# Row statistics of x from a token-major copy on ScalarE, first loads in another order, products of ones ahead of the data

## The chip, the cores and the metric

The kernel runs on one core of one Trainium2 chip. The metric is the device time in microseconds (us) of that core. A profile is one execution taken by the hardware profiler. Its span runs from the first to the last instruction. The engines are TensorE (PE, with its weight loads as PEld), VectorE (DVE), ScalarE (ACT), GpSimd (POOL) and SyncE (SP), which here only issues DMAs.

## The reference, cut to what matters

One block of a streaming encoder works on x of 256 tokens by 2048 features, in float32. Only its start bears on this change:

```
def rms_norm(x, g):
    y = x * lax.rsqrt(jnp.mean(x * x, axis=-1, keepdims=True) + EPS)
    return y * g

h = rms_norm(x, norm_mix_pre)
proj = h @ w_in                      # 2048 -> 20544 columns
q, k, v, z, xbc, dt, g_sb, g_ssd = split(proj)
```

After it come a stick-breaking attention, a Mamba-2 scan, their gated merge, an output projection, and a gated MLP with a width-3 convolution, each with the same kind of norm.

## The kernel before, in words

All large products are of float32 quality, made of three float32r passes: every operand is split into hi (the rounded value) and lo (the exact rest). The weights come as 713 units of 128 x 1024 floats (512 KB). For unit u SyncE loads `raw`u (five buffers), ScalarE casts it to `whi`u (line 63), VectorE subtracts to get `wlo`u (line 64), each with five buffers, and TensorE consumes both. So ScalarE can write `whi`u only when TensorE is done with unit u-5, and SyncE can load `raw`u only when VectorE is done with `wlo`(u-5).

The gain of the norm is multiplied into x, but 1/rms is applied to the products behind. So the first products need no statistics. x comes feature-major (`xT`) in four chunks of 512 KB, `x0` to `x3`. For each chunk ScalarE makes the hi half (line 188, four instructions of 128x256) and VectorE the lo half (line 189, four), both in `a`0 to `a`3. These and the splits of units 0 to 7 stand in a block whose order on ScalarE and VectorE is as written.

TensorE then runs `first`: four column tiles at once (`feat_mms`, lines 123 to 130), chunk by chunk. Per chunk two units are used. A unit gives 8 pairs of matmuls: hi weights by the 512 columns of hi and lo (line 112), lo weights by the 256 columns of hi (line 113). That makes 64 pairs for `first`, then 16 for each following column tile (`ps_xs`, `ps_bc`). After those come `ps_z` and the rest.

The statistics: GpSimd squares each chunk (line 197), adds the squares up (line 201) and folds them twice (line 203), nine instructions in all. Two small matmuls with ones (line 395, `ss_x`) sum over the partitions. `rsqrt_mean` (lines 237 to 242, names `rx_...`) makes 1/rms per token on VectorE and ScalarE. `tok_to_bc` spreads it over the partitions: `rx_dg` on VectorE, the matmul `rx_ps` (line 250) on TensorE behind the first `ps_xs` tile, and the copy `rstd_bc` (line 251) on VectorE. The convolutions (lines 311 to 315) and the dt path (lines 260 to 298) need `rstd_bc`.

Within one engine and one queue all work goes in order. Outside the blocks written as such, a scheduler sets that order.

Of the kernel before, what the change touches and what calls it, by code (L numbers as in the profile page):

```python
# [10 lines left out]
F32 = mybir.dt.float32  # L11
# [27 lines left out]
def block_kernel(ctx, tc, xT, xN, wts, vecs, rows, hvec, dskip, gain, out):  # L39
    """Float32 products run as three float32r passes on hi + lo halves (hi the rounded value, lo the  # L40
    exact rest) of both operands. Weights come in units [128, 8 x 128] and are split on chip."""
    nc = tc.nc
# [15 lines left out]
    def act_chunk(name):  # L58
        """four k tiles of an operand [feature, token]: hi and lo beside each other"""
        return slot(F32R, [4, 2, T], name)  # L60
# [5 lines left out]
    def lnexp():  # L66
        """the table set that serves both Ln and Exp"""
        tc.keep_in_program_order(nc.scalar.preload_act_table_set(LNEXP))

# [1 line left out]
    raw_t, spl_t = {}, {}  # L71
# [9 lines left out]
    def prep(parts=1):  # L81
        """split the next unit of weights, a part per step"""
        v = state["u"]
        state["u"] += 1
        if v not in raw_t:
            load(v)
        raw = raw_t.pop(v)
        hi = wspl.tile([P, 1024], F32R, tag="whi", name=f"whi{v}")
        lo = wspl.tile([P, 1024], F32R, tag="wlo", name=f"wlo{v}")
        spl_t[v] = (hi, lo)  # L90
        n = 1024 // parts
        for i in range(parts):
            w = slice(i * n, (i + 1) * n)
            split(hi[:, w], lo[:, w], raw[:, w])
            yield

    def unit(ahead=WBUFS - 2):
        """the next unit's hi and lo; the units after it are prepared ahead"""
        u = state["at"]
        state["at"] += 1  # L100
        while state["u"] <= min(u + ahead, n_units - 1):
            for _ in prep():
                pass
        return spl_t.pop(u)
# [4 lines left out]
    def feat_tile(ps, hi, lo, c, act, k, last):  # L109
        """one weight tile into out[feature 128, token 256]; columns 256: take hi x lo"""  # L110
        w = slice(c * P, (c + 1) * P)
        nc.tensor.matmul(ps, hi[:, w], act[:, k % 4, :, :].rearrange("p s t -> p (s t)"), start=(k == 0), stop=last)  # L112
        nc.tensor.matmul(ps[:, :T], lo[:, w], act[:, k % 4, 0, :], start=False, stop=last, skip_group_check=True)  # L113
# [9 lines left out]
    def feat_mms(acts, pss):  # L123
        """several column tiles together, so that each chunk of the operand is used for longer"""
        for kc in range(4):
            for i, ps in enumerate(pss):
                if i % 2 == 0:
                    hi, lo = unit()
                for k in range(4):
                    feat_tile(ps, hi, lo, 4 * (i % 2) + k, acts[kc], 4 * kc + k, 4 * kc + k == KT - 1)  # L130
# [5 lines left out]
    def tok_mm(acts, nk, name):  # L136
        """out[token 128, feature 512] for both token tiles"""
        pss = [mm_bank(f"{name}_{t}") for t in range(2)]
        for k in range(nk):
            if k % 2 == 0:  # L140
                hi, lo = unit()
            w = slice(k % 2 * 512, k % 2 * 512 + 512)
            for t in range(2):
                ah, al = (acts[k // 4][:, k % 4, s, t * P:(t + 1) * P] for s in range(2))
                nc.tensor.matmul(pss[t], ah, hi[:, w], start=(k == 0), stop=False)  # L145
                nc.tensor.matmul(pss[t], ah, lo[:, w], start=False, stop=False)  # L146
                nc.tensor.matmul(pss[t], al, hi[:, w], start=False, stop=(k == nk - 1))  # L147
            if k % 4 == 3:
                pump()
        return pss  # L150

# [1 line left out]
    bg = []  # L153
# [11 lines left out]

# [1 line left out]
    gpre = const.tile([P, KT], F32, name="gpre")  # L167
# [3 lines left out]
    for c in range(4):  # L171
        xr = slot(F32, [4, T], f"x{c}")
        nc.sync.dma_start(xr, xT[:, 4 * c:4 * c + 4, :])
        for u in range(2 * c, min(2 * c + 2, RBUFS)):
            load(u, 2 if u == 0 else 1)
        x_raw.append(xr)
    nc.sync.dma_start(vec, vecs[:, KT:])
    hv = const.tile([64, 2], F32, name="hv")
    nc.sync.dma_start(hv, hvec)

    with tc.manual_schedule(engines=ACT_DVE):
        lnexp()
        for c in range(4):
# [10 lines left out]
            a_ch.append(ac)  # L194
            sqc = slot(F32, [4 * T], f"xsq{c}")
            xf_c = x_raw[c].rearrange("p k t -> p (k t)")
            nc.gpsimd.tensor_tensor(sqc, xf_c, xf_c, op=ALU.mult)
            if c == 0:
                xsq = sqc
            else:  # L200
                nc.gpsimd.tensor_tensor(xsq, xsq, sqc, op=ALU.add)
    for n in (512, 256):
        nc.gpsimd.tensor_tensor(xsq[:, :n], xsq[:, :n], xsq[:, n:2 * n], op=ALU.add)

# [1 line left out]
    dsk = const.tile([P, 64], F32, name="dsk")  # L206
    nc.gpsimd.dma_start(dsk, dskip.partition_broadcast(P))
    ident = const.tile([P, P], F32, name="ident")
    make_identity(nc, ident)
    ones = const.tile([P, P], F32, name="ones")  # L210
    nc.gpsimd.memset(ones, 1.0)

# [20 lines left out]
    def rsqrt_mean(dst, src, n, name):  # L233
        """1 / sqrt(src / n + EPS) of [128, 2], with a Newton step"""
        v = tmp.tile([P, 2], F32, tag="rs_v", name=f"{name}_v")
        q = tmp.tile([P, 2], F32, tag="rs_q", name=f"{name}_q")
        nc.vector.tensor_scalar(v, src, 1.0 / n, EPS, op0=ALU.mult, op1=ALU.add)
        nc.scalar.activation(q, v, AF.Ln)
        nc.scalar.activation(dst, q, AF.Exp, scale=-0.5)
        nc.vector.tensor_tensor(q, dst, dst, op=ALU.mult)  # L240
        nc.vector.scalar_tensor_tensor(q, q, -0.5, v, op0=ALU.mult, op1=ALU.mult)
        nc.vector.scalar_tensor_tensor(dst, q, 1.5, dst, op0=ALU.add, op1=ALU.mult)

    def tok_to_bc(dst, src, pool, tag, name):
        """dst[p, token] = src[token] on every partition"""
        dg = tmp.tile([P, T], F32, tag="diag", name=f"{name}_dg", bufs=1)
# [5 lines left out]

# [1 line left out]
    cs_dram = dram.tile([64, T], F32, name="cs_dram")  # L254
# [44 lines left out]

# [1 line left out]
    y_ch = []  # L301
# [86 lines left out]
    def to_feat(ch, t, src, pool, tag, name):  # L388
        """src [token 128, 512] into the operand chunk ch [feature, token]"""
        split_chunk(ch, t, transposed(src, pool, tag, f"{name}_{t}"))  # L390

    def stats_x():
        ps = paux.tile([P, 512], F32, tag="aux", name="ss_x")
        for t in range(2):
            nc.tensor.matmul(ps[:, t:t + 1], xsq[:, t * P:(t + 1) * P], ones[:, 0:1], start=True, stop=True)
        rsqrt_mean(rstd_tok, ps[:, 0:2], 2048, "rx")

# [34 lines left out]

# [1 line left out]
    def gate(dst, name):  # L434
# [14 lines left out]

# [1 line left out]
    tmp = work.enter_context(tc.tile_pool(name="tmp_d", bufs=2))  # L451
# [10 lines left out]
    def attn_work(hg, qk, vt):  # L462
        """columns of a pair of heads: 0:512 = head, query (keys 0:128); 512:768 = head, query 128: (keys 128:)"""
        oc = act_chunk(f"o{hg}")
# [64 lines left out]

# [1 line left out]
    gat = [slot(F32, [2048], f"gat{t}") for t in range(2)]  # L531
# [21 lines left out]

# [1 line left out]
    xn = [slot(F32, [2048], f"xn{t}") for t in range(2)]  # L555
# [14 lines left out]
    class PostNorm:  # L570
        """the statistics of a normalised output that comes in four column blocks"""

# [77 lines left out]

# [1 line left out]
    r2 = const.tile([P, T], F32, name="r2")  # L652
# [74 lines left out]
def _m_tiles(w):  # L727
    """[k, n] -> [n / 128, 128, k / 128, 128]: a block per 128 columns, k's partition first"""
    k, n = w.shape
# [3 lines left out]
def _m_units(w):  # L733
    """units of 8 k tiles, column tile by column tile"""
    m = _m_tiles(w)
# [4 lines left out]
def _joint_units(w):  # L740
    """units of 4 k tiles of two column tiles, all column tiles' first, then all their second, ..."""
    m = _m_tiles(w)
# [4 lines left out]
def _n_units(w):  # L747
    """units of 2 k tiles by 512 columns: [n / 512, k / 256, 128, 1024]"""
    k, n = w.shape
# [3 lines left out]
def _cols(v):  # L753
    """[n] or [r, n] -> [128, n / 128 * r]: per partition, the r values of each tile"""
    v = v.reshape(-1, v.shape[-1])
# [50 lines left out]
```

## Time and profile before

| what | value |
|---|---|
| times of three runs | 2110.87, 2111.7, 2121.52 us (median 2111.7) |
| span of the profiled execution | 2109.0 us |
| TensorE busy | 2069.9 us (98%) |
| VectorE busy | 1399.9 us (66%) |
| ScalarE busy | 1154.5 us (55%) |
| GpSimd busy | 172.1 us (8%) |
| moved by DMA | 400.70 MB, mean 190 GB/s |

The profile gives a span and no other time for the execution that it records, so that span is set against the times of the runs. The busy shares are means over the whole program. The change lies in its first 50 us.

### The profile page before, as it was taken

What the parts mean: (1) busy time and instruction counts of PE and PEld (TensorE: products, weight loads), DVE (VectorE), ACT (ScalarE), POOL (GpSimd) and SP (SyncE); (2) the same over time, 40 slices, a digit from 0 to 9 for tenths busy, and PEclk for the clock granted to TensorE, in tenths of its full rate; (3) what the DMA queues carried; (4) which work ended last, traced back from release to release, by engine and by line L of the source; (5) the groups of instructions that cost most, each with busy time, mean ns of one, the idle gap of its engine ahead of it and who ended that gap; (6) DMA issues with size and microseconds to landing.
All of it is one profiled execution on the core that took longest, in us unless ns stands there. A gap on an engine that the chain in (4) does not pass through costs nothing.

```text
span 2109.0 us, 27916 instructions
## 1 busy us (share of the span) xinstructions
PE 2069.9 (98%) x10616; PEld 1761.4 (84%) x10616; DVE 1399.9 (66%) x1793; ACT 1154.5 (55%) x1538; POOL 172.1 (8%) x144
## 2 busy tenths in 40 slices
PE   7999999999999999999999999999999999999997
PEld 6788888888888888888888888788888888888886
DVE  8887877888544445555554566598788878854443
ACT  4776777677543334555556444475555555544442
POOL 4221012221000000000000021100000000000000
PEclk9999999999999999999999999999999999999999
DMA  6555555655655555555555746465565555566653
GB/s 237 178 186 189 201 185 176 210 171 181 191 195 193 193 196 188 182 170 170 170 174 183 272 162 208 150 239 190 190 189 191 190 190 190 190 230 199 200 192 108
DMA packets 108662, 400.70 MB, mean 190 GB/s; under 512 B 12368, under 2 KB 12624, under 8 KB 106480
## 3 DMA queue, kind: packets, MB, share of 16 engines
q1 hardware_dynamic: 104480, 377.97, 54.5%
q0 software_dynamic: 3328, 20.02, 2.7%
q8 instruction: 83, 1.36, 0.3%
q10 hardware_dynamic: 720, 0.93, 0.1%
q14 instruction: 51, 0.42, 0.1%
HBM read 394.61 MB, written 4.26 MB: 189 GB/s over the span
## 4 chain that ended last, share of the span: by engine, by line
PE 91%; DVE 3%; POOL 2%; issue 2%; ACT 1%; DMA 1%; SPq 0%; DVEq 0%; ACTq 0%; POOLq 0%
PE ps_fg L112 7%; PE ps_fv L112 7%; PE ps_qk L112 6%; PE ps_xs L112 5%; PE ps_fv L113 4%; PE ps_fg L113 4%; PE ps_fo L146 4%; PE ps_fo L147 4%; PE ps_fo L145 4%; PE ps_qk L113 3%; PE ps_ssd L147 3%; PE ps_ssd L145 3%; PE ps_ssd L146 3%; PE ps_xs L113 3%; PE ps_bc L112 2%
## 5 line engine op out<-in xcount | busy, mean ns | idle before, releaser
L64 DVE TENSOR_TENSOR wlo<-raw,whi 128x1024 fp32r<-128x1024 f32 (+1 forms) x715 | 908.8, 1276 | 601.1 <-ACT whi L63 600.7
L63 ACT CAST whi<-raw 128x1024 fp32r<-128x1024 f32 (+1 forms) x715 | 746.8, 1051 | 811.1 <-PE ps_fo L147 128.9
L112 PE MATMUL ps_fg<-h,whi 128*128 128x512 f32 x688 | 240.7, 391 | 0.0
L112 PE MATMUL ps_fv<-h,whi 128*128 128x512 f32 x688 | 240.5, 391 | 0.0
L113 PE MATMUL ps_fv<-h,wlo 128*128 128x256 f32 x688 | 192.7, 280 | 0.0
L113 PE MATMUL ps_fg<-h,wlo 128*128 128x256 f32 x688 | 192.7, 280 | 0.0
L112 PE MATMUL ps_qk<-a,whi 128*128 128x512 f32 x512 | 181.3, 398 | 0.0
L112 PE MATMUL ps_xs<-a,whi 128*128 128x512 f32 x464 | 162.9, 396 | 0.0
L112 PEld LDWEIGHTS ps_fg<-h,whi 128*128 128x128 f32 x688 | 128.7, 187 | 28.3
L112 PEld LDWEIGHTS ps_fv<-h,whi 128*128 128x128 f32 x688 | 128.7, 187 | 28.3
L113 PE MATMUL ps_qk<-a,wlo 128*128 128x256 f32 x512 | 143.5, 280 | 0.0
L147 PE MATMUL ps_fo<-whi,f 128*128 128x512 f32 x352 | 136.9, 389 | 0.0
L146 PE MATMUL ps_fo<-wlo,f 128*128 128x512 f32 x352 | 136.9, 389 | 0.0
L145 PE MATMUL ps_fo<-whi,f 128*128 128x512 f32 x352 | 136.9, 389 | 0.0
L113 PEld LDWEIGHTS ps_fg<-h,wlo 128*128 128x128 f32 x688 | 130.0, 189 | 0.0
L113 PEld LDWEIGHTS ps_fv<-h,wlo 128*128 128x128 f32 x688 | 130.0, 189 | 0.0
L113 PE MATMUL ps_xs<-a,wlo 128*128 128x256 f32 x464 | 129.0, 278 | 0.0
L112 PEld LDWEIGHTS ps_qk<-a,whi 128*128 128x128 f32 x512 | 96.1, 188 | 22.6
L145 PE MATMUL ps_z<-whi,a 128*128 128x512 f32 x256 | 103.6, 406 | 0.0
L112 PEld LDWEIGHTS ps_xs<-a,whi 128*128 128x128 f32 x464 | 87.0, 188 | 19.5
L146 PE MATMUL ps_z<-wlo,a 128*128 128x512 f32 x256 | 100.5, 393 | 1.0 <-DVE wlo L64 1.0
L147 PE MATMUL ps_z<-whi,a 128*128 128x512 f32 x256 | 100.1, 391 | 0.0
(283 smaller groups left out, 3853.3 us busy)
## 6 DMA issues: line engine op xcount, KB each, us to landing
raw<-wts SPq DMA_DIRECT2D x713, 512.0 KB, 3.8
csb<-cs_dram POOLq DMA_DIRECT2D x8, 1024.0 KB, 7.8
x<-xT SPq DMA_DIRECT2D x4, 512.0 KB, 9.0
csb<-gain POOLq DMA_DIRECT2D x8, 256.0 KB, 4.3
xn<-xN POOLq DMA_DIRECT2D x2, 1024.0 KB, 8.1
x_dram<-xn POOLq DMA_DIRECT2D x2, 1024.0 KB, 9.2
xe<-x_dram POOLq DMA_DIRECT2D x2, 1024.0 KB, 10.3
gfo<-rows POOLq DMA_DIRECT2D x4, 256.0 KB, 5.0
```

The lines of the kernel that those rows point to most:

```text
L63: nc.scalar.copy(hi, src)
L64: nc.vector.tensor_tensor(lo, src, hi.bitcast(F32), op=ALU.subtract)
L112: nc.tensor.matmul(ps, hi[:, w], act[:, k % 4, :, :].rearrange("p s t -> p (s t)"), start=(k == 0), stop=last)
L113: nc.tensor.matmul(ps[:, :T], lo[:, w], act[:, k % 4, 0, :], start=False, stop=last, skip_group_check=True)
L145: nc.tensor.matmul(pss[t], ah, hi[:, w], start=(k == 0), stop=False)
L146: nc.tensor.matmul(pss[t], ah, lo[:, w], start=False, stop=False)
L147: nc.tensor.matmul(pss[t], al, hi[:, w], start=False, stop=(k == nk - 1))
```

## The change

The nine squares and sums on GpSimd and the two `ss_x` matmuls go. Instead x is loaded once more, token-major (`xN`, two tiles `xt0`, `xt1` of 1 MB, 128 tokens each), on SyncE's queue. ScalarE squares each tile in place with a row sum (`accum_out`), one instruction of 128x2048 per tile. `rsqrt_mean` takes these sums.

The first loads come in another order: half of `x0`, half of unit 0, the other halves, unit 1, then `x1` and the rest as before. The loads of `vec` and `hv` are written behind the block of splits.

The constant `ones` is set by VectorE at the very start, and TensorE multiplies it by itself ten times (`wake`, float32, 128 columns each) into a bank that nobody reads. The diff also deletes comments, which moves line numbers; those parts are left out here.

```diff
...
+    ones = const.tile([P, P], F32, name="ones")
+    nc.vector.memset(ones, 1.0)
+    wake = paux.tile([P, 512], F32, tag="aux", name="wake")
+    for i in range(10):
+        nc.tensor.matmul(wake[:, :P], ones, ones, start=True, stop=True)
     gpre = const.tile([P, KT], F32, name="gpre")
     nc.scalar.dma_start(gpre, vecs[:, 0:KT])
     vec = const.tile([P, C_N - KT], F32, name="vec")
     a_ch, x_raw = [], []
     for c in range(4):
-        xr = slot(F32, [4, T], f"x{c}")
-        nc.sync.dma_start(xr, xT[:, 4 * c:4 * c + 4, :])
+        x_raw.append(slot(F32, [4, T], f"x{c}"))
+    raw0 = wraw.tile([P, 1024], F32, tag="raw", name="raw0")
+    raw_t[0] = raw0
+    for i in range(2):
+        nc.sync.dma_start(x_raw[0][:, 2 * i:2 * i + 2, :], xT[:, 2 * i:2 * i + 2, :])
+        nc.sync.dma_start(raw0[:, i * 512:i * 512 + 512], wts[0][:, i * 512:i * 512 + 512])
+    load(1)
+    for c in range(1, 4):
+        nc.sync.dma_start(x_raw[c], xT[:, 4 * c:4 * c + 4, :])
         for u in range(2 * c, min(2 * c + 2, RBUFS)):
-            load(u, 2 if u == 0 else 1)
-        x_raw.append(xr)
-    nc.sync.dma_start(vec, vecs[:, KT:])
-    hv = const.tile([64, 2], F32, name="hv")
-    nc.sync.dma_start(hv, hvec)
+            load(u)
...
             a_ch.append(ac)
-            sqc = slot(F32, [4 * T], f"xsq{c}")
-            xf_c = x_raw[c].rearrange("p k t -> p (k t)")
-            nc.gpsimd.tensor_tensor(sqc, xf_c, xf_c, op=ALU.mult)
-            if c == 0:
-                xsq = sqc
-            else:
-                nc.gpsimd.tensor_tensor(xsq, xsq, sqc, op=ALU.add)
-    for n in (512, 256):
-        nc.gpsimd.tensor_tensor(xsq[:, :n], xsq[:, :n], xsq[:, n:2 * n], op=ALU.add)
+    nc.sync.dma_start(vec, vecs[:, KT:])
+    hv = const.tile([64, 2], F32, name="hv")
+    nc.sync.dma_start(hv, hvec)
+    x_tok = [slot(F32, [2048], f"xt{t}") for t in range(2)]
+    for t in range(2):
+        nc.sync.dma_start(x_tok[t], xN[t * P:(t + 1) * P, :])
...
     def stats_x():
-        ps = paux.tile([P, 512], F32, tag="aux", name="ss_x")
-        for t in range(2):
-            nc.tensor.matmul(ps[:, t:t + 1], xsq[:, t * P:(t + 1) * P], ones[:, 0:1], start=True, stop=True)
-        rsqrt_mean(rstd_tok, ps[:, 0:2], 2048, "rx")
+        ss = tmp.tile([P, 2], F32, tag="ss", name="ss_x")
+        for t in range(2):
+            nc.scalar.activation(x_tok[t], x_tok[t], AF.Square, accum_out=ss[:, t:t + 1])
+        rsqrt_mean(rstd_tok, ss, 2048, "rx")
```

On SyncE's queue, behind the first five units. Before, the weight units follow one another:

```order
L78 DMA raw7_184<-wts 128x1024
L78 DMA raw8_308<-wts 128x1024
L78 DMA raw9_330<-wts 128x1024
L78 DMA raw10_352<-wts 128x1024
L78 DMA raw11_401<-wts 128x1024
```

And now:

```order
L78 DMA raw7_187<-wts 128x1024
L78 DMA raw8_311<-wts 128x1024
L208 DMA xt0_197<-xN 128x2048
L208 DMA xt1_198<-xN 128x2048
L78 DMA raw9_333<-wts 128x1024
L78 DMA raw10_355<-wts 128x1024
```

The two tiles of x stand between the loads of units 8 and 9; `vec` and `hv` keep their place ahead of unit 5.

On ScalarE at the end of `first`, with the casts of units 8 to 13, the copies of the four finished tiles (`dts`, `cvr`) and the two steps of `rsqrt_mean`. Before:

```order
L63 CAST whi8_310<-raw8_308 128x1024
L63 CAST whi9_332<-raw9_330 128x1024
L63 CAST whi10_354<-raw10_352 128x1024
L133 COPY dts_223<-ps_first0_224 64x256
L63 CAST whi11_403<-raw11_401 128x1024
L133 COPY cvr0_376<-ps_first1_225 128x256
L133 COPY cvr1_379<-ps_first2_226 128x256
L63 CAST whi12_425<-raw12_423 128x1024
L133 COPY cvr2_382<-ps_first3_227 128x256
L238 ACTIVATE rx_q_389<-rx_v_388 128x2
L239 ACTIVATE rstd_tok_216<-rx_q_389 128x2
L63 CAST whi13_507<-raw13_505 128x1024
```

And now:

```order
L63 CAST whi8_313<-raw8_311 128x1024
L398 ACTIVATE xt0_197,ss_x_388<-xt0_197 128x2048
L398 ACTIVATE xt1_198,ss_x_388<-xt1_198 128x2048
L63 CAST whi9_335<-raw9_333 128x1024
L133 COPY dts_226<-ps_first0_227 64x256
L241 ACTIVATE rx_q_392<-rx_v_391 128x2
L63 CAST whi10_357<-raw10_355 128x1024
L133 COPY cvr0_379<-ps_first1_228 128x256
L242 ACTIVATE rstd_tok_219<-rx_q_392 128x2
L63 CAST whi11_406<-raw11_404 128x1024
L133 COPY cvr1_382<-ps_first2_229 128x256
L63 CAST whi12_428<-raw12_426 128x1024
```

The two row sums stand between the casts of units 8 and 9, so those of units 9 and later are queued behind them.

On VectorE at the same place, with the splits, the sums of the finished tiles and the `rx_...` steps up to `rx_dg`. Before:

```order
L64 TENSOR_TENSOR wlo11_404<-raw11_401,whi11_403 128x1024
L134 TENSOR_TENSOR cvr0_376<-cvr0_376,ps_first1_225 128x256
L134 TENSOR_TENSOR cvr1_379<-cvr1_379,ps_first2_226 128x256
L237 TENSOR_SCALAR rx_v_388<-ss_x_385 128x2
L64 TENSOR_TENSOR wlo12_426<-raw12_423,whi12_425 128x1024
L134 TENSOR_TENSOR cvr2_382<-cvr2_382,ps_first3_227 128x256
L240 TENSOR_TENSOR rx_q_389<-rstd_tok_216 128x2
L241 SCALAR_TENSOR_TENSOR rx_q_389<-rx_q_389,rx_v_388 128x2
L242 SCALAR_TENSOR_TENSOR rstd_tok_216<-rx_q_389,rstd_tok_216 128x2
L249 TENSOR_SCALAR rx_dg_445<-ident_198,rstd_tok_216 128x128 x2
```

And now:

```order
L64 TENSOR_TENSOR wlo9_336<-raw9_333,whi9_335 128x1024
L134 TENSOR_TENSOR dts_226<-dts_226,ps_first0_227 64x256
L64 TENSOR_TENSOR wlo10_358<-raw10_355,whi10_357 128x1024
L134 TENSOR_TENSOR cvr0_379<-cvr0_379,ps_first1_228 128x256
L243 TENSOR_TENSOR rx_q_392<-rstd_tok_219 128x2
L64 TENSOR_TENSOR wlo11_407<-raw11_404,whi11_406 128x1024
L134 TENSOR_TENSOR cvr1_382<-cvr1_382,ps_first2_229 128x256
L244 SCALAR_TENSOR_TENSOR rx_q_392<-rx_q_392,rx_v_391 128x2
L64 TENSOR_TENSOR wlo12_429<-raw12_426,whi12_428 128x1024
L134 TENSOR_TENSOR cvr2_385<-cvr2_385,ps_first3_230 128x256
L245 SCALAR_TENSOR_TENSOR rstd_tok_219<-rx_q_392,rstd_tok_219 128x2
L252 TENSOR_SCALAR rx_dg_448<-ident_203,rstd_tok_219 128x128 x2
```

The `rx_...` steps are now spread between the splits of units 9 to 12. The next two instructions, the split of unit 13 and `rstd_bc`, stand as before, and from there on the order is the same in both kernels on every engine.

## Rows read from the trace of the kernel before

**Rows 1.** Busy time of the engines in stretches of the span (windows).

```profile
core 0: us, PE busy (x) PEld busy (x) DVE busy (x) ACT busy (x) POOL busy (x), PEclk, DMA share, GB/s
...
20.00:30.00 10.00, 5.98 (x26) 5.20 (x27) 10.00 (x7) 4.16 (x7) 9.06 (x5) 0.66 0.30 105
30.00:40.00 10.00, 9.85 (x57) 8.30 (x56) 10.00 (x13) 3.53 (x4) 0.00 (x0) 1.00 0.65 202
...
110.00:2109.00 1999.00, 1978.42 (x10143) 1684.85 (x10141) 1309.27 (x1667) 1085.40 (x1439) 136.77 (x112) 1.00 0.58 189
```

**Rows 2.** TensorE's timeline: start, us, engine, line, operation [idle before <-releaser].

```profile
10.32 0.63 PE L112 MATMUL ps_first<-a,whi 128*128 128x512 f32 x1
...
24.02 0.58 PE L113 MATMUL ps_first<-a,wlo 128*128 128x256 f32 x1 [7.59 <-DVE wlo L64]
...
31.79 0.39 PE L112 MATMUL ps_first<-a,whi 128*128 128x512 f32 x1
...
42.74 0.50 PE L395 MATMUL ss_x<-ones,xsq 128*128 128x1 f32 x4
43.10 0.48 PE L112 MATMUL ps_xs<-a,whi 128*128 128x512 f32 x1
...
48.74 0.59 PE L250 MATMUL rx_ps<-rx_dg,ones 128*128 128x256 f32 x2
```

**Rows 3.** VectorE's timeline.

```profile
10.79 1.23 DVE L64 TENSOR_TENSOR wlo<-raw,whi 128x1024 fp32r<-128x1024 f32 x1 [1.03 <-ACT whi L63]
11.94 9.19 DVE L189 SCALAR_TENSOR_TENSOR a<-x,gpre,a 128x256 fp32r<-128x256 f32 x4
21.05 6.22 DVE L64 TENSOR_TENSOR wlo<-raw,whi 128x1024 fp32r<-128x1024 f32 x2
...
32.57 1.66 DVE L189 SCALAR_TENSOR_TENSOR a<-x,gpre,a 128x256 fp32r<-128x256 f32 x4
34.15 5.75 DVE L64 TENSOR_TENSOR wlo<-raw,whi 128x1024 fp32r<-128x1024 f32 x5
...
49.37 0.42 DVE L251 COPY rstd_bc<-rx_ps 128x256 f32<-128x256 f32 x1 [1.01 <-PE rx_ps L250]
49.90 1.23 DVE L64 TENSOR_TENSOR wlo<-raw,whi 128x1024 fp32r<-128x1024 f32 x1
```

**Rows 4.** GpSimd's timeline, first and last of the nine instructions on squares.

```profile
4.80 1.89 POOL L197 TENSOR_TENSOR xsq<-x 128x1024 f32<-128x1024 f32 x1 [0.59 <-DMA x<-xT]
...
26.27 3.03 POOL L203 TENSOR_TENSOR xsq<-xsq 128x512 f32<-128x512 f32 x2
```

**Rows 5.** ScalarE's timeline, the rows that waited for a transfer.

```profile
9.71 1.04 ACT L63 CAST whi<-raw 128x1024 fp32r<-128x1024 f32 x1 [0.68 <-DMA raw<-wts]
10.99 1.71 ACT L188 ACTIVATE a<-x,gpre 128x256 fp32r<-128x256 f32 x4 [0.23 <-DMA x<-xT]
...
14.82 1.71 ACT L188 ACTIVATE a<-x,gpre 128x256 fp32r<-128x256 f32 x4 [0.22 <-DMA x<-xT]
...
19.53 1.04 ACT L63 CAST whi<-raw 128x1024 fp32r<-128x1024 f32 x1 [2.06 <-DMA raw<-wts]
```

**Rows 6.** ScalarE's groups over the whole program: count | busy, mean ns | idle.

```profile
L63 ACT CAST whi<-raw 128x1024 fp32r<-128x1024 f32 x713 | 745.6, 1053 | 809.8 <-PE ps_fo L147 128.9 <-PE ps_ssd L147 106.0 <-PE ps_fv L112 96.8
...
L344 ACT ACTIVATE mm<-mm 128x2048 f32<-128x2048 f32 x8 | 15.3, 1915 | 34.5 <-POOL mm L336 34.5
...
L133 ACT COPY cvr<-ps_first 128x256 f32<-128x256 f32 x3 | 1.1, 367 | 0.1
```

**Rows 7.** Line 366, ScalarE's Square with a row sum: ns min/median/max.

```profile
L366 ACT ACTIVATE xs<-xs x16: 626/632/639, 107.4 to 542.6; 128x512 f32<-128x512 f32 x16
L366 ACT ACTIVATION_READ_ACCUMULATOR xs<-xs x16: 184/186/196, 107.9 to 543.2; 128x1 f32 x16
```

**Rows 8.** The chain of waits, 28 to 112 us: start, us, what.

```profile
48.82 1.06 ACT whi L63
...
66.16 1.15 DVE wlo L64
```

More of the change, by code (lines that the diff above doesn't have):

```diff
@@ L209, in block_kernel @@
     make_identity(nc, ident)
-    ones = const.tile([P, P], F32, name="ones")
-    nc.gpsimd.memset(ones, 1.0)
     def tri(name, src, base, cm, step, pool=const):
```

## The prediction, blind

> **What bounds the kernel now.** I read the stretches first: what happens in the first 50 us, and what behind them? From 110 us to the end TensorE is busy for 1978.42 of 1999 us [rows 1], and the change touches nothing there. What it can win lies ahead of that. In TensorE's timeline the reader is to see one large hole: at 24.02 it had been idle for 7.59 us, waiting for VectorE's split of unit 2 [rows 2]. From 31.79 on it runs without a gap to the end of `first` at 42.74: 31 pairs in 10.95 us, 0.353 us a pair [rows 2].
>
> Why was that split late? VectorE's timeline answers. The four lo halves of chunk 1 took 9.19 us from 11.94, the next two splits 6.22 us. Later the same work takes 1.66 us for four and 5.75 us for five splits, 1.15 each [rows 3]. What differs is GpSimd: its nine instructions on squares run from 4.80 to 29.30 [rows 4], and VectorE is at its usual speed once they are over. So VectorE loses 7.5 us on the four lo halves and 3.9 us on the two splits to them.
>
> The clock adds to it. A 512-column matmul takes 0.63 us at 10.32 and 0.39 us at 31.79 [rows 2]; between 20 and 30 us the granted clock is 0.66 on average, a stretch partly at 1.2 GHz after the hole, and 1.00 from 30 us on [rows 1].
>
> The transfers set the earliest times. ScalarE waited for unit 1 until 9.71, `x1` until 10.99, `x2` until 14.82 and unit 5 until 19.53 [rows 5]. Between `x1` and `x2` lie units 2 and 3 and `x2` itself, three loads of 512 KB in 3.83 us: 1.28 us each, in the order of issue.
>
> From 48.82 on the chain of waits leaves TensorE and goes over ScalarE and VectorE (the cast and split of unit 14, then convolutions and dt) to another split at 66.16 [rows 8]. So the gain has to be counted at two points: where TensorE starts `ps_xs` (43.10) [rows 2], and where VectorE reaches `rstd_bc` (49.37) and the split of unit 14 (49.90) [rows 3]. The later one decides.
>
> **Part 1: the squares leave GpSimd.** Unit 1 lands when it did, since the same bytes stand ahead of it: 9.71. Its split ends at 12.02 as before [rows 3]. The four lo halves of chunk 1 then take 1.66 us (to 13.7) and the split of unit 2 takes 1.15 (to 14.85), instead of after 24.
>
> TensorE: the last 8 of chunk 0's 16 pairs need unit 1's split at 12.0, so they end at 12.0 + 8 x 0.353 = 14.85. From there 48 pairs take 16.95 us, to 31.8, if nothing waits. The splits due on the way, in VectorE's order: unit 3 at 16.0 (needed at 17.7); `x2` at 14.82, its hi halves to 16.5, lo halves to 17.7, unit 4 at 18.9 (needed at 20.5); unit 5, landing 19.53, cast to 20.6, split to 21.75 (needed at 23.3); lo halves of chunk 3 to 23.4; units 6, 7 and 8 at 24.6, 25.7 and 26.9 (needed at 26.15, 28.95 and 31.8). Each has 1.4 us or more to spare. The two `ss_x` matmuls, 43.10 - 42.74 = 0.36 us, are gone. So `ps_xs` starts at 31.8 instead of 43.10: 11.3 us earlier.
>
> **Part 2: the statistics by ScalarE.** Their price is a later transfer and work queued on ScalarE. SyncE issues `xt0` and `xt1` behind unit 8, whose load waits for the split of unit 3 (16.0); the transfers are then still behind. At 1.28 us per 512 KB units 6, 7 and 8 land at 20.8, 22.1 and 23.4, `xt0` (1 MB) at 25.9, `xt1` at 28.5, unit 9 at 29.8. No row shows a row sum of 128x2048. From below there is an activation of that size without the sum, 1.92 us [rows 6]; from above four of 128x512 with their read-out, 4 x (0.63 + 0.19) = 3.3 us [rows 7]. I take 1.92 + 0.19 = 2.1, since the row of the same size is the nearer. The sums end at 28.0 and 30.6 (32.5 with the upper bound: both sums run back to back).
>
> Behind them on ScalarE waits the cast of unit 9: to 31.65, its split to 32.9. TensorE needs it at 34.6, so it does not stall there. But VectorE, idle from 26.9, then has a queue up to `rx_dg`: three splits (3.5), four sums of `first` tiles (about 0.37 each as on ScalarE [rows 6], 1.5) and the small `rx` steps (1.1): 6.1 us, to 39.0. TensorE would be ready for `rx_ps` at 31.8 + 16 x 0.353 = 37.45. It waits 1.5 us and runs it at 39.0 instead of 48.74: 9.7 earlier. The split of unit 13 (1.15) stands ahead of `rstd_bc`, which comes at 40.1 instead of 49.37, and the split of unit 14 at 40.5 instead of 49.90: 9.4 us earlier. From there the order is the old one, on engines that all are at least 9.4 us ahead, so the later stages move as a whole.
>
> A rule that would put the tiles later is in the Trainium skill, "DMA: Bandwidth & Descriptors", section Specifications: it gives HBM about 358 GB/s per core. An estimate by that page: units 5 to 8 and both tiles, 4.2 MB, would take 11.7 us instead of 10.3, the gain falls to about 8.0 us. The trace here has 512 KB in 1.28 us, 410 GB/s [rows 5], so it does not bear that out.
>
> **Part 3: the order of the first loads.** The halves change what lands first within 1 MB; unit 1 still comes behind the same bytes. The start of chunk 0 may move by up to 0.6 us either way (half a 512 KB load). It counts for nothing, since unit 1's split at 12.0 decides when chunk 0 ends. If that cover goes (unit 1 earlier), it is a gain of the same size.
>
> **Part 4: ten products of ones.** The nearest row is `rx_ps`, float32 with 256 columns, 0.59 us in all [rows 2]. So ten of half the width take at most 5.9 us at full clock, 11.8 at half, and nothing at least, as TensorE has no data then. I take about 6 us, over by 7 to 8. They cost nothing as long as they end before about 12.0, where unit 1 is due. What they can give is full clock for chunk 0; that too is hidden behind the split at 12.0, except that the last 8 pairs at half clock (0.63 against 0.39, about 0.29 us more a pair) would end 2.3 us later. Of these, 1.5 us are covered by TensorE's wait for `rx_dg`.
>
> **The sum.** -9.4 us against a span of 2109.0: 2099.6. The median lies 2.7 us above the span, so 2102.3 us.
>
> **The rivals.**
> - TensorE sets the end alone. If the tiles land about 2 us earlier, VectorE keeps pace and the whole 11.3 us come through: 2100.4. For it: every row of VectorE past the squares is at full speed. Against: SyncE's order, by which the tiles are behind unit 8.
> - The tiles land later, or share the transfers with units 9 to 11 (three times 1.28, 3.8 us). Each us counts in full, as VectorE's queue starts at the cast of unit 9: 2103.8 to 2106.1. Against: rows 5, by which loads land in turn.
> - The clock is at its lower level over chunk 0 and beyond, in spite of the products: 1 to 2 us beyond the cover, about 2104. For it: before, matmuls were still slow at 10.32, over 3 us after data came.
> - The change doesn't do what it says: the slow VectorE rows come from the transfers or ScalarE and not from the squares. Then only the clock's part is left, 10 pairs by 0.29: about 2108.7. Against: the lo halves are fast from 29.3 on while loads and ScalarE go on.
> - Slower: the row sums stop ScalarE, which goes in order, so no weight is cast until `xt1` is there. This eats the whole gain when `xt1` lands at 28.5 + 9.4 = 37.9 or later, 2.1 MB in 14.5 us, 145 GB/s. At 40 us it gives 2113.8. Against: 410 GB/s in rows 5.
>
> **How the numbers follow.** Forecast 0.60 (gain 8.3 to 10.9), TensorE alone 0.19, later tiles 0.11, clock 0.03, squares not the cause 0.04, slower 0.03. The range 2099.8 to 2106.3 takes in the first four. Half a per cent, about what a measurement of this kernel can tell from no change, is 10.6 us, so 2101.1: below it lie TensorE alone and about 0.08 of the forecast's upper edge, 0.27. Above 2122.3 lies at most 0.02. The rest, 0.71, is within half a per cent: the likeliest gain is real but just under that bound.
>
> **What would show it.** The four lo halves of chunk 1 in about 1.7 us; no hole of several us on TensorE at 16 us; `ps_xs` starting near 31.8; the row sums of about 2.1 us each, the second ending near 30.6, with ScalarE waiting for `xt1` ahead of it; TensorE waiting about 1.5 us for `rx_dg`; `rstd_bc` near 40.1. It is wrong if VectorE's rows stay at 2 us and more, or if a new hole of over 3 us opens before 110 us.

## The result, and the profile after

The median went from 2111.28 us to 2101.95 us (four runs each). The ratio is 0.9946, with an interval of 0.9924 to 0.9967. It lies below the ratio of the medians, 0.9956, and the kernel before has slower runs: over all measurements 16 of its 41 runs took 2118 us or more, none of the 39 runs of a kernel without the squares took over 2105.6, and no profile here shows one of the 16. The forecast was 2102.3. The profiled execution has a span of 2099.6 us and took 2101.31 us; the spans of the other three runs are 2100.2 to 2100.7.

The stretches after, in the columns of [rows 1]. The first row has no counterpart there: it is the stretch in which TensorE works on chunk 0.

```profile
9.00:16.00 7.00, 6.05 (x20) 5.20 (x21) 5.59 (x10) 5.96 (x11) 0.00 (x0) 0.53 1.03 415
20.00:30.00 10.00, 10.00 (x59) 8.69 (x58) 6.22 (x8) 7.60 (x11) 0.00 (x0) 1.00 1.02 413
30.00:40.00 10.00, 10.00 (x59) 8.64 (x58) 7.08 (x15) 8.00 (x13) 0.00 (x0) 1.00 0.73 272
110.00:2099.00 1989.00, 1969.82 (x10092) 1674.10 (x10090) 1301.45 (x1653) 1077.43 (x1427) 136.72 (x112) 1.00 0.57 189
```

From 20 to 30 us TensorE is busy throughout, where it was at 5.98 of 10 us. But from 9 to 16 us its granted clock is 0.53 on average, so nearly all of this stretch is at 1.2 GHz. VectorE's timeline after, which answers to [rows 3]:

```profile
11.91 1.23 DVE L64 TENSOR_TENSOR wlo<-raw,whi 128x1024 fp32r<-128x1024 f32 x1 [0.91 <-ACT whi L63]
13.05 1.67 DVE L197 SCALAR_TENSOR_TENSOR a<-x,gpre,a 128x256 fp32r<-128x256 f32 x4
14.79 2.36 DVE L64 TENSOR_TENSOR wlo<-raw,whi 128x1024 fp32r<-128x1024 f32 x2
...
31.94 0.17 DVE L240 TENSOR_SCALAR rx_v<-ss_x 128x2 f32<-128x2 f32 x1 [3.96 <-ACT xt L398]
32.88 1.23 DVE L64 TENSOR_TENSOR wlo<-raw,whi 128x1024 fp32r<-128x1024 f32 x1 [0.77 <-ACT whi L63]
...
39.15 0.48 DVE L252 TENSOR_SCALAR rx_dg<-ident,rstd_tok 128x128 f32<-128x128 f32 x2
39.74 1.23 DVE L64 TENSOR_TENSOR wlo<-raw,whi 128x1024 fp32r<-128x1024 f32 x1
40.88 0.42 DVE L254 COPY rstd_bc<-rx_ps 128x256 f32<-128x256 f32 x1
41.28 1.23 DVE L64 TENSOR_TENSOR wlo<-raw,whi 128x1024 fp32r<-128x1024 f32 x1
```

The four lo halves of chunk 1 take 1.67 us, not 9.19, and the next two splits 2.36, not 6.22. VectorE then idles 3.96 us for the second row sum. `rstd_bc` comes at 40.88 and the split of unit 14 at 41.28, 8.5 and 8.6 us earlier. TensorE's timeline, which answers to [rows 2]:

```profile
1.12 4.47 PE L171 MATMUL wake<-ones 128*128 128x128 f32 x20 [1.12 <-DVE ones L168]
6.34 0.50 PE L112 MATMUL ps_first<-a,whi 128*128 128x512 f32 x1 [0.76 <-DVE a L197]
...
9.95 0.79 PE L112 MATMUL ps_first<-a,whi 128*128 128x512 f32 x1 [2.13 <-DVE a L197]
...
14.59 0.63 PE L112 MATMUL ps_first<-a,whi 128*128 128x512 f32 x1
...
34.46 0.40 PE L112 MATMUL ps_xs<-a,whi 128*128 128x512 f32 x1
40.11 0.59 PE L253 MATMUL rx_ps<-rx_dg,ones 128*128 128x256 f32 x2
```

The hole of 7.59 us is gone. A small one is new: after the first two pairs TensorE waits 2.13 us for the second half of `x0`, and then runs 512-column matmuls in 0.63 us until 15.2. ScalarE's timeline, which answers to [rows 5] and shows the row sums:

```profile
8.87 0.91 ACT L196 ACTIVATE a<-x,gpre 128x256 fp32r<-128x256 f32 x2 [2.58 <-DMA x<-xT]
...
10.84 1.04 ACT L63 CAST whi<-raw 128x1024 fp32r<-128x1024 f32 x1 [0.55 <-DMA raw<-wts]
...
20.69 1.05 ACT L63 CAST whi<-raw 128x1024 fp32r<-128x1024 f32 x1 [2.06 <-DMA raw<-wts]
...
29.90 1.92 ACT L398 ACTIVATE xt<-xt 128x2048 f32<-128x2048 f32 x1 [0.53 <-DMA xt<-xN]
31.73 0.18 ACT L398 ACTIVATION_READ_ACCUMULATOR xt<-xt 128x1 f32 x1
```

Unit 1 is cast at 10.84, not at 9.71 as before, and unit 5 at 20.69, not 19.53. The whole stream of loads comes about 1.1 us later.

### The profile page after: what moved, and what is told of

It is laid out like the page before. It is cut to its first block, busy times and chain, and to the rows that moved or that the text cites. A ratio compares the mean times of both kernels' runs of the same rounds, so it can differ in the third digit from the quotient of the medians.

```text
span 2099.6 us, 27950 instructions
## 1 busy us (share of the span) xinstructions
PE 2072.1 (99%) x10632; PEld 1760.7 (84%) x10632; DVE 1386.0 (66%) x1794; ACT 1156.9 (55%) x1542; POOL 152.3 (7%) x134
## 4 chain that ended last, share of the span: by engine, by line
PE 92%; POOL 2%; DVE 2%; issue 2%; DMA 1%; ACT 1%; SPq 0%; DVEq 0%; ACTq 0%; POOLq 0%
PE ps_fv L112 8%; PE ps_fg L112 8%; PE ps_qk L112 6%; PE ps_xs L112 5%; PE ps_fo L147 4%; PE ps_fo L145 4%; PE ps_fo L146 4%; PE ps_fg L113 4%; PE ps_fv L113 4%; PE ps_qk L113 3%; PE ps_ssd L147 3%; PE ps_ssd L145 3%; PE ps_ssd L146 3%; PE ps_xs L113 2%; PE ps_bc L112 2%; PE ps_z L146 2%
```

## The experiments

The theory after the result: GpSimd's squares held VectorE, and their removal gives the whole gain. After it the landing of the second token-major tile sets `rstd_bc`, and that landing is late because the first loads run slowly. Rivals: the gain comes from the products of ones or the new load order; or the loads are late for a reason other than their order. Ratios below are to the kernel before, run beside each.

**e1: the squares back beside the changed kernel.**

```
     for c in range(4):
...
+        nc.gpsimd.tensor_tensor(sqc, xf_c, xf_c, op=ALU.mult)
...
+            nc.gpsimd.tensor_tensor(xsq, xsq, sqc, op=ALU.add)
+    for n in (512, 256):
+        nc.gpsimd.tensor_tensor(xsq[:, :n], xsq[:, :n], xsq[:, n:2 * n], op=ALU.add)
```

> The changed kernel with the nine GpSimd squares and sums put back beside the new row sums; nothing reads what they write. Theory (the squares slow VectorE): the four lo halves of chunk 1 take 6 us or more instead of 1.7, the splits of units 2 and 3 over 2 us each, TensorE has a hole of several us in chunk 1, and most of the gain is gone: rstd_bc near 48 to 50 instead of 40.9, the time within 2 us of the kernel before. Rival (the transfers or ScalarE slowed VectorE before, or the order of loads cured it): the lo halves stay at about 1.7 us, no hole, rstd_bc near 41, the time near 2102.

Measured: 2113.38 us, ratio 0.9992 (0.9973 to 1.0011): the gain is gone. VectorE, GpSimd and TensorE in its timeline:

```profile
13.39 9.19 DVE L197 SCALAR_TENSOR_TENSOR a<-x,gpre,a 128x256 fp32r<-128x256 f32 x4
22.50 6.21 DVE L64 TENSOR_TENSOR wlo<-raw,whi 128x1024 fp32r<-128x1024 f32 x2
...
12.34 2.89 POOL L205 TENSOR_TENSOR xsq<-x 128x1024 f32<-128x1024 f32 x1 [1.29 <-DMA x<-xT]
15.30 2.47 POOL L209 TENSOR_TENSOR xsq<-xsq,xsq 128x1024 f32<-128x1024 f32 x1
17.74 2.07 POOL L205 TENSOR_TENSOR xsq<-x 128x1024 f32<-128x1024 f32 x1
19.89 2.41 POOL L209 TENSOR_TENSOR xsq<-xsq,xsq 128x1024 f32<-128x1024 f32 x1
...
25.46 0.58 PE L113 MATMUL ps_first<-a,wlo 128*128 128x256 f32 x1 [6.97 <-DVE wlo L64]
```

The same 9.19 us and a hole of 6.97 us are back, and `rstd_bc` comes at 50.16, though nothing but these nine instructions was added. The four lo halves span the four GpSimd instructions above, and one VectorE instruction gets through per GpSimd instruction. One by one they take 2.12, 2.63, 2.11 and 2.56 us, not 0.4, and each ends about 0.3 us behind the GpSimd instruction beside it. That agrees with the Trainium skill, "SBUF — State Buffer", section "SBUF: two separate sides": a VectorE instruction with two operands in SBUF and a GpSimd instruction that reads SBUF exclude each other for a whole instruction.

**e5: the statistics alone.** The kernel before with Part 1 and Part 2 only: loads in the old order, no products of ones.

```
-            nc.gpsimd.tensor_tensor(sqc, xf_c, xf_c, op=ALU.mult)
...
+    for t in range(2):
+        nc.sync.dma_start(x_tok[t], xN[t * P:(t + 1) * P, :])
...
+            nc.scalar.activation(x_tok[t], x_tok[t], AF.Square, accum_out=ss[:, t:t + 1])
```

> The kernel before with the statistics alone changed (row sums on ScalarE from the token-major copy): loads in the old order, no products of ones, dsk where it was. Theory (this part holds all of the gain): no hole on TensorE, unit 1 cast near 9.7, rstd_bc near 40 to 40.5, a time within 1 us of the changed kernel's 2102. Rival (the loads and the products carry part of it): rstd_bc at 42 or later, the time 2 us or more above 2102.

Measured: 2101.68 us, ratio 0.9926 (0.9901 to 0.9952). VectorE, and ScalarE at the second row sum, in its timeline:

```profile
11.85 1.67 DVE L191 SCALAR_TENSOR_TENSOR a<-x,gpre,a 128x256 fp32r<-128x256 f32 x4
...
29.54 1.92 ACT L392 ACTIVATE xt<-xt 128x2048 f32<-128x2048 f32 x1 [1.82 <-DMA xt<-xN]
...
40.49 0.42 DVE L248 COPY rstd_bc<-rx_ps 128x256 f32<-128x256 f32 x1
```

Unit 1 is cast at 9.63 and `rstd_bc` comes at 40.49. The statistics alone give the gain; the other two parts add nothing to it that can be measured.

**e2: the old order of loads in the changed kernel.**

```
-    for i in range(2):
-        nc.sync.dma_start(x_raw[0][:, 2 * i:2 * i + 2, :], xT[:, 2 * i:2 * i + 2, :])
-        nc.sync.dma_start(raw0[:, i * 512:i * 512 + 512], wts[0][:, i * 512:i * 512 + 512])
+    nc.sync.dma_start(x_raw[0], xT[:, 0:4, :])
+    load(0, 2)
```

> The changed kernel with the first loads in the old order (x0 whole, then the two halves of unit 0). Theory (the order by halves makes the whole stream of loads 1.1 us late): unit 1 is cast at 9.7 instead of 10.84, xt1 lands at 28.8 instead of 29.9, the second half of x0 is there before 6 us so TensorE has no hole of 2 us after its first pairs, rstd_bc comes near 39.8 instead of 40.9, and the time is 1 to 2 us below the changed kernel's. Rival (the loads were late by chance or from something else, such as the dsk broadcast): unit 1 is cast near 10.8 and the time stays.

Measured: 2101.38 us, ratio 0.9925 (0.9897 to 0.9952). The difference to the changed kernel, 0.6 us, is less than was expected and inside the intervals; the trace tells more than the time:

```profile
9.59 1.05 ACT L63 CAST whi<-raw 128x1024 fp32r<-128x1024 f32 x1 [0.66 <-DMA raw<-wts]
...
29.18 1.92 ACT L395 ACTIVATE xt<-xt 128x2048 f32<-128x2048 f32 x1 [0.51 <-DMA xt<-xN]
...
31.37 0.39 PE L112 MATMUL ps_xs<-a,whi 128*128 128x512 f32 x1
38.95 0.96 PE L250 MATMUL rx_ps<-rx_dg,ones 128*128 128x256 f32 x2 [1.88 <-DVE rx_dg L249]
...
40.12 0.42 DVE L251 COPY rstd_bc<-rx_ps 128x256 f32<-128x256 f32 x1
```

These are close to the forecast's own numbers: unit 1 9.71, `ps_xs` 31.8, `rx_ps` 39.0 after a wait of 1.5 us, `rstd_bc` 40.1. So the forecast's picture of TensorE left the trace at the order of the first loads. That `rx_ps` comes out so near is partly luck: the second sum ends 0.6 us later than forecast, at 31.18, and the queue behind it is 0.6 us shorter.

**e3: no products of ones.**

```
-    for i in range(10):
-        nc.tensor.matmul(wake[:, :P], ones, ones, start=True, stop=True)
```

> The changed kernel without the ten products of ones. Theory (the products raise the clock for the first two pairs only, then a hole of 2 us without data lets it fall): chunk 0 is at the lower clock up to about 15 as it is with the products, ps_xs starts within 1 us of 34.5, the time is the same within 1 us. Rival (the products pay): ps_xs starts 2 us or more later and the time rises by as much.

Measured: 2102.15 us, ratio 0.9924 (0.9900 to 0.9948). `ps_xs` starts at 32.67, earlier than with the products (34.46) and outside the 1 us that was expected; `rstd_bc` comes at 40.67. Eight pairs are slow in both kernels, but here two of them run ahead of the hole and six behind it. The loads are also 0.7 us earlier in this one execution (unit 1 at 10.10), which removing the products does not explain. In time the products give nothing.

**e4: the broadcast of `dsk` later.** GpSimd's load of `dskip`, spread over 128 partitions, is issued at 1.3 us in all kernels above and first read at 72.3 us in the changed kernel. Here it waits for a copy that VectorE writes into `dsk` behind the statistics of x, and is issued at 37.2 us.

```
-    nc.gpsimd.dma_start(dsk, dskip.partition_broadcast(P))
...
     stats_x()
+    nc.vector.tensor_copy(dsk[:, 0:2], rstd_tok)
+    nc.gpsimd.dma_start(dsk, dskip.partition_broadcast(P))
```

> The changed kernel with the broadcast load of dsk on GpSimd's queue held until the row statistics are there (by a write of VectorE to its tile first). Theory (its slow packets between 4.5 and 7 us hold up the first loads): the dip in what the transfers move between 4 and 6 us (155 GB/s in the changed kernel) goes, the second half of x0 lands before 7 instead of 8.87, unit 1 is cast before 10 instead of 10.84, all later loads are 1 us or more earlier and the time falls by 1 to 2 us. Rival (the order by halves alone is the cause): the dip stays or unit 1 is still cast near 10.8.

Measured: 2099.65 us (2098.50 to 2099.84), ratio 0.9913 (0.9882 to 0.9944), the lowest median of the study, though e8's is only 0.07 us above it. The transfers of 4.5 to 7 us, queue by queue (packets, MB, share of 16 engines), first in the changed kernel and then in e4:

```profile
DMA packets 215, 0.43 MB, mean 174 GB/s; under 512 B 30, under 2 KB 30, under 8 KB 215
q1 hardware_dynamic: 201, 0.42, 69.2%
q0 software_dynamic: 14, 0.01, 15.9%
```

```profile
DMA packets 270, 0.67 MB, mean 267 GB/s; under 512 B 31, under 2 KB 31, under 8 KB 270
q1 hardware_dynamic: 270, 0.67, 88.4%
```

And e4's timeline:

```profile
8.61 1.05 ACT L63 CAST whi<-raw 128x1024 fp32r<-128x1024 f32 x1 [0.61 <-DMA raw<-wts]
...
27.53 1.92 ACT L397 ACTIVATE xt<-xt 128x2048 f32<-128x2048 f32 x1 [0.51 <-DMA xt<-xN]
...
30.68 0.40 PE L112 MATMUL ps_xs<-a,whi 128*128 128x512 f32 x1
37.30 0.70 PE L252 MATMUL rx_ps<-rx_dg,ones 128*128 128x256 f32 x2 [0.81 <-DVE rx_dg L251]
...
38.30 0.42 DVE L253 COPY rstd_bc<-rx_ps 128x256 f32<-128x256 f32 x1
```

The rate in these 2.5 us goes from 174 to 267 GB/s, unit 1 comes 2.2 us earlier than in the changed kernel, and `rstd_bc` 2.6 us earlier. So a broadcast of 0.03 MB held up the first megabyte. The other kernels bear this out. In the six that issue it at 1.3 us (the kernel before, the changed one, e1, e2, e3, e5) all transfers move 132 to 184 GB/s between 4.5 and 7 us; in the four that hold it back (e4, e6, e7, e8) 267 to 349. This window can miss its packets: in e3 they take 0.2% of it, as they start earlier. From 3 to 7 us they take 22 to 36% of the DMA engines' time in each of the six.

**e8: e4 with the old order of loads.** The edit of e2, made on e4.

```
-    for i in range(2):
...
+    nc.sync.dma_start(x_raw[0], xT[:, 0:4, :])
+    load(0, 2)
```

> The changed kernel with dsk held back and the first loads in the old order. Theory (the order by halves costs time only because the second half of x0 falls among the slow packets of dsk; without them the order is worth nothing either way): unit 1 cast within 0.4 us of 8.61, rstd_bc within 0.5 us of 38.3, time within 0.7 us of 2099.65. Rival (the order by halves is worth or costs 1 us of itself): unit 1 or rstd_bc moves by 1 us or more.

Measured: 2099.72 us, ratio 0.9927 (0.9900 to 0.9953). Unit 1 is cast at 8.03, 0.6 us earlier than in e4 where at most 0.4 was expected; `rstd_bc` comes at 38.38. With e2 and e4 this makes a square. Unit 1's cast, old order against halves in turn: 9.59 against 10.84 with the broadcast early, 8.03 against 8.61 with it late. So the new order costs 0.6 us by itself and 1.25 beside the broadcast, and the broadcast costs 1.6 and 2.2. Each corner is one execution, but other kernels repeat it: 9.71 and 9.63 (the kernel before, e5) for the first, 11.00 and 10.10 (e1, e3) for the second, 8.18 (e6) for the third and 8.62 (e7) for the fourth. So the cost beside the broadcast is uncertain, 0.4 to 1.4 us; the others agree within 0.2. At `rstd_bc` the broadcast costs 1.7 and 2.6 us, and the order nothing by itself (38.30 against 38.38) and 0.8 beside the broadcast (0.2 by e3 and e5, which have no products).

**e7: e4 without the products of ones.** The edit of e3, made on e4.

```
-        nc.tensor.matmul(wake[:, :P], ones, ones, start=True, stop=True)
```

> The changed kernel with dsk held back, and without the products of ones. Theory (without a hole behind them the products keep the clock up for chunk 0, but VectorE's queue sets rstd_bc, so little of it counts): chunk 0 runs partly at the lower clock, ps_xs 0 to 1.5 us later than 30.7, the wait for rx_dg shrinks from 0.8, rstd_bc within 0.5 us of 38.3, the time within 0.7 us of 2099.65. Rival (the products pay once the data come without a hole): rstd_bc and the time 1 us or more later.

Measured: 2100.36 us, ratio 0.9932 (0.9908 to 0.9955), 0.71 us above e4. `ps_xs` starts at 31.24, 0.56 us later than in e4, as matmuls run in 0.63 us until 10.5. `rstd_bc` comes at 38.38, 0.08 later. Here the products do bring the higher clock earlier, and it still gives nothing that can be measured, because TensorE waits for `rx_dg` behind it in both (0.33 and 0.81 us).

**e6: the kernel before with only the broadcast late.** The edit of e4, made on the kernel before.

```
-    nc.gpsimd.dma_start(dsk, dskip.partition_broadcast(P))
...
+    nc.vector.tensor_copy(dsk[:, 0:2], rstd_tok)
+    nc.gpsimd.dma_start(dsk, dskip.partition_broadcast(P))
```

> The kernel before with nothing but the broadcast of dsk held back. Theory (the squares on GpSimd set the end of this stretch, so earlier loads win little): unit 1 is cast before 9.2 instead of 9.71, the lo halves of chunk 1 still take over 8 us, the hole on TensorE stays at 6 to 8 us, rstd_bc comes 0.5 to 1.5 us earlier than 49.37 and the time falls by 0 to 1.5 us. Rival (the 2 us that the late dsk gave the changed kernel are independent of the squares): the time falls by 2 us or more.

Measured: 2113.1 us, ratio 0.9986 (0.9965 to 1.0007). TensorE's hole in its timeline:

```profile
22.66 0.58 PE L113 MATMUL ps_first<-a,wlo 128*128 128x256 f32 x1 [7.52 <-DVE wlo L64]
```

Unit 1 is cast at 8.18, 1.5 us earlier, but the hole is still 7.52 us long and `rstd_bc` comes at 48.50, only 0.87 earlier. While the squares set the pace, faster loads are worth nothing that can be measured.

## Why the prediction was right, and where its terms were off

The forecast missed the median by 0.4 us, and its mechanism holds: VectorE's queue behind the second row sum sets the gain. The size came out closer than its terms deserve: the tiles came 1.3 us late, the queue behind them was 0.7 us shorter, and 0.9 us came from a place that the forecast did not look at.

- **Part 1, the squares: right.** 1.67 us for the lo halves against 1.66 forecast; e1 shows that the squares and nothing else made them slow, and e5 that their removal, with the new statistics, is all of the gain. The rivals "squares not the cause" and "slower" fall. The rival "later tiles" came true in part, by 1.3 us at the end of the second sum.
- **"Unit 1 lands when it did, since the same bytes stand ahead of it": wrong, 10.84 for 9.71.** The bytes are the same, but the second half of `x0` now stands behind the first half of unit 0, and the transfers are at their slowest just then. e2 brings 9.59 back. The bound of 0.6 us for Part 3 rested on loads at full rate; beside the broadcast the order cost 1.25 in this execution (0.4 to 1.4 over the repeats), and from there the tiles are late too.
- **The row sums: size right, place 1.3 us late.** 1.92 + 0.18 us each against 2.1. The second ends at 31.91, forecast 30.6. In e2, with unit 1 on time, it still ends at 31.18: 0.6 us of the miss is the estimate of when `xt1` lands (29.18 for 28.5), the rest the load order. In e5, also in the old order, `xt1` lands only at 29.54, so how the miss is shared between the two is known to 0.4 us.
- **The queue up to `rx_dg`: 0.7 us too long.** The forecast has 8.4 us from the end of the second sum to the end of `rx_dg`. It is 7.7 us (31.91 to 39.63), in e2 and e4 too. No single term was much too large: the small `rx` steps, `rx_dg` among them, take 0.87 us for 1.1, the four sums 1.33 for 1.5, the cast and split of unit 9 take 2.1 for 2.3, the three splits 3.4 for 3.5.
- **TensorE: no wait for `rx_dg`, where 1.5 us was forecast.** `ps_xs` starts at 34.46, not 31.8. Behind the hole of 2.13 us the clock falls, and eight pairs run at the lower level, as the forecast had feared of a cold start. This is what its rival on the clock describes, chance 0.03, but not at that rival's price. The forecast had said that most of this is covered, and here all of it is: `rx_ps` ends at 40.70 (40.11 + 0.59), before VectorE is through with the split ahead of `rstd_bc` (40.88).
- **Part 4, the products: right in effect.** They take 4.47 us, forecast about 6, and end at 5.59. That they give nothing is what e3 and e7 measured.
- **The sum: -8.5 us at `rstd_bc`, forecast -9.3.** The profiled span is exactly the forecast 2099.6, but that is luck, as the forecast did not count a part of it. From `rstd_bc` to the end it is 2059.6 us in the kernel before and 2058.7 in this execution. These 0.9 us lie far behind the change, at `r_ps`, where the 1/rms of the MLP's norm is spread over the partitions. Before (the group's row: busy, mean ns, idle) and after:

```profile
L250 PE MATMUL r_ps<-r_dg,ones 128*128 128x256 f32 x2 | 0.7, 417 | 0.8 <-DVE r_dg L249 0.8
```

```profile
1380.97 0.60 PE L253 MATMUL r_ps<-r_dg,ones 128*128 128x256 f32 x2
```

In the kernel before and in e6, ScalarE waits 1.1 us for a weight load just ahead of it, and TensorE then 0.8 us for `r_dg`. The changed kernel and the seven experiments with the new statistics, e1 among them, have neither wait. So the 0.9 us come with the new statistics and not with this one execution, and the later stages did not quite "move as a whole". Why the load is late there is not shown.
- **The spans of the experiments hold a term of their own.** They run 2059.7 to 2061.1 us from `rstd_bc` to the end. At `po`, the scan's first product of this kind, TensorE waits for GpSimd's `xw`; before, after and in e4:

```profile
86.37 1.12 PE L350 MATMUL po<-xw 128*128 128x512 f32 x2 [2.48 <-POOL xw L333]
```

```profile
77.64 1.13 PE L353 MATMUL po<-xw 128*128 128x512 f32 x2 [2.39 <-POOL xw L336]
```

```profile
74.98 1.63 PE L352 MATMUL po<-xw 128*128 128x512 f32 x2 [2.38 <-POOL xw L335]
```

The wait is 2.4 to 2.5 us in all ten profiles, but in the eight experiments the granted clock falls to 1.2 GHz for a stretch there (0.89 to 0.90 on average from 75 to 90 us), and in the two profiles before and after it does not (1.00). From `rstd_bc` to the first of the transposes that follow (`pt`) it is 69.0 to 69.3 us with the fall and 67.8 to 67.9 without it. So single spans differ by over 1 us for a reason outside the change, and `rstd_bc` is the surer measure of it.
- **From the span to the time: 2.7 us, 1.7 of them found in every run.** Wherever a run's span is on record, its time is 1.7 to 1.8 us longer. By that, the other 1.0 us is how much faster the profiled execution of the kernel before was than its median run; after, that difference is 0.6.

What ties all the versions without squares together: `rstd_bc` follows the start of the second row sum by 10.8 to 11.0 us in every one (29.90 to 40.88 here; 29.18 to 40.12 in e2, 29.70 to 40.67 in e3, 27.53 to 38.30 in e4, 29.54 to 40.49 in e5, 27.61 to 38.38 in e7, 27.55 to 38.38 in e8). The clock, the order of the loads and the broadcast move TensorE's `ps_xs` by up to 3.8 us and this distance by 0.2. So in these kernels the gain follows from when that tile lands.

What stays open: why the loads of e3 came 0.7 us earlier, how much of 0.6 us in time the load order costs, and why the kernel before waits for a load at `r_ps`.

## What to carry to other kernels

When an engine is slow in one stretch and at its usual speed in another, look at what its neighbours do in the slow stretch before blaming its input; one run with the suspected work put back beside the change settles it. When the first loads decide, look at each small transfer that shares the first microseconds with them and ask when its data are needed. A reordering of loads that moves the same bytes need not be free: what matters is which transfer is in the queue while the rate is low, and who waits for it.

## What the runs showed of the hardware

- A load of 0.03 MB spread over 128 partitions can cost the loads beside it far more than its bytes. It lands 5.8 us after its issue in the changed kernel. Between 3 and 7 us its packets take 22 to 36% of the DMA engines' time in the six kernels that issue it at 1.3 us, and all transfers together move 197 to 219 GB/s; the four that hold it back move 295 to 337. From 9 to 16 us the changed kernel moves 415.
- VectorE instructions with two operands in SBUF and GpSimd's squares went by turns: 2.1 to 2.6 us for a lo half that takes 0.4 alone (e1).
- Products of ones raised TensorE's clock in each kernel that has them, but it stayed up only where data followed soon. With holes of 0.81, 0.50 and 0.57 us (e2), or of 0.52 and less (e4), all of chunk 0 but e4's first pair runs at 2.4 GHz. With a hole of 2.13 us (the changed kernel), or with 1.56 us ahead of the first product of data (e8), the clock falls back to 1.2 GHz, and eight pairs or about four are slow. Behind the wait of 2.4 to 2.5 us at `po` (about 75 to 87 us) the clock fell in eight executions and stayed up in two.
- ScalarE's row sum over 2048 columns costs 1.92 us, the same as the activation of that size without a sum, and 0.18 us to read it out.
